# The value products of two query tiles in one run, and the transposes three units behind the scores, in an encoder's attention stage

## The chip, the core and the metric

The kernel runs on one core of one Trainium2 chip. The metric is the device time of one execution in microseconds (us), as the median of several runs. Engines: PE is the matmul engine (TensorE) and PEld its weight loads, DVE is VectorE, ACT is ScalarE, POOL is GpSimd, and SP is the queue from which most DMAs are issued.

## What is computed

One layer of an encoder for two request groups (1024 and 256 tokens of width 1024): modulated norm, one input projection, two attention branches side by side, a gated merge, an output projection, and a mixture of 32 experts. The change lies in the attention branches, 8 heads of width 64 each:

```python
sc = (jnp.einsum('bqhd,bkhd->bhqk', qn, k_nope, preferred_element_type=jnp.float32)
      + jnp.einsum('bqhr,bkr->bhqk', qr, k_rope, preferred_element_type=jnp.float32))
p = jax.nn.softmax(sc * scale, axis=-1).astype(v.dtype)
return jnp.einsum('bhqk,bkhd->bqhd', p, v)
```

That is the latent branch ("m"): every query of a group sees all its keys. The neighbourhood branch ("n") has a bias table and sees only a window of keys: for a tile of 128 queries, 384 columns of keys hold it, or 256 at the two ends.

## The kernel before, in words

**Units.** The attention stage is a list of 160 units. A unit is one head (x = 0 or 1 of a pair), one tile of 128 queries (qi) and all the keys that this tile sees. Units 0 to 63 are the m branch of the long group (1024 columns each), 64 to 127 its n branch (384 columns, 256 for qi 0 and 7), 128 to 159 the short group (256 columns, m and n by turns). Sixteen units (8 query tiles by 2 heads) use the tiles of one job, which holds queries, keys, values and bias tables and is loaded by `Job.load` (L807 to L857).

**What a unit does.** `scores` (PE, L895) fills one of two PSUM buffers. `maximum` (DVE, L903 for m, L907 with the bias for n) takes the row maximum, `exp` (ACT, L913) the exponentials and their sum, `normalize` the reciprocal (DVE, L916) and the scaling (POOL, L917). `transpose` (PE, L927; copies back by ACT and DVE, L929) turns the probabilities round, 128 columns at a time. `pv` (PE, L945) multiplies those of the two heads of a pair by the values: the two heads write the two halves of the PE array (64 columns each), by turns, 16, 12 or 8 products of 128 columns in each head-pair run of m, interior n or narrow units. The trace has two PE records per product. When the odd query tile is done, ACT (L951) and DVE (L952) split the product tile in two, and SP stores it (L954).

**Order.** No scheduler is at work: each engine executes in the order in which the loop below emits. In turn i it emits scores and maximum of unit i, transposes of unit i - LOOK, exp and normalize of unit i, then `pv`, then the loads that a table has for this i, then 2 or 3 matmuls of a filler. The filler (`piece_gates`) is the gate projection of the first 512 tokens, 16 groups of 24 matmuls (L678); at the end of a group ACT copies the result (L682) and SP stores it (L683), and about every nine units ACT and DVE split the next weights in two (L654, L655). The filler is used up at unit 145.

**Slots.** All tiles of 128x1024 come from one first-in-first-out list of 49 slots (`sl.get`, `sl.put`). A put is made when the last use has been emitted, not when it is done; so whoever gets a slot waits for its last reader, which may be a store that is still in flight. A unit's probabilities hold a slot from `maximum` to `pv`.

The loop reads, before:

```python
if u:
    u.exp()
    u.normalize()
if z and z.x:
    pv(units[i - LOOK - 2], z)
```

Of the kernel before, what the change touches and what calls it, by code (L numbers as in the profile page):

```python
# [86 lines left out]
def f32(x):  # L87
    return x.bitcast(F32)


def v3(t, k):
    return t.rearrange("p (k n) -> p k n", k=k)
# [3 lines left out]
def kernel(ctx, tc, A, out_p, out_s, upto=99, dbg=None):  # L96
# [311 lines left out]
    def work(g, *after):  # L408


        gi = order.index(g)
        def ahead():
            if gi + 1 < len(order):
                order[gi + 1].split()
            if gi + 2 < len(order):
                order[gi + 2].load()

        g.run(ahead)
        ada_step()
        for f in after:  # L420
            f()
            ada_step()
        g.put()
# [371 lines left out]
    def fill(n):  # L795

        while filled[0] < n:
            filled[0] += 1
            if next(fill_it, True):
                break  # L800
# [132 lines left out]
    def pv(a, b):  # L933

        half = a.qi % 2
        key = (a.kind, a.p, a.job.g)
        if half == 0:
            oacc[key] = fps["o"][:, oturn[0] % 2, :]
            oturn[0] += 1
        o = oacc[key]  # L940
        cs = slice(half * 128, half * 128 + 128)
        for i in range(0, a.n, 128):
            w = min(128, a.n - i)
            for u in (a, b):
                PE.matmul(o[64 * u.x:64 * u.x + 64, cs], u.job.vat(u.t0 + i // 128, u.h, w), v3(u.P, 8)[:w, i // 128, :],  # L945
                          start=(i == 0), stop=(i + 128 >= a.n), tile_position=(0, 64 * u.x), skip_group_check=True)
        sl.put(a.P, b.P)
        if half:
            os = sl.get(F32R)
            t = os[:, :512].rearrange("p (x n) -> p x n", x=2)  # L950
            S.copy(t[:, 0], o)  # L951
            V.tensor_sub(t[:, 1], o, f32(t[:, 0]))  # L952
            tk = (SP if a.job.g else 0) + (a.qi - 1) * 128
            SY.dma_start(ao_d[a.kind][:, a.p * 128:a.p * 128 + 128, tk:tk + 256].rearrange("x r n -> r x n"), f32(t))  # L954
            sl.put(os)
        if b.last:
            sl.put(*b.job.t)

    jobs = [Job(kind, 0, p) for kind in "mn" for p in range(4)]
    units = []  # L960
# [4 lines left out]
    for i in range(2):  # L965
        sj = [Job(kind, 1, i) for kind in "mn"]
        jobs += sj
        seqs = [[Unit(j, p, qi, x) for p in (2 * i, 2 * i + 1) for qi in range(2) for x in range(2)] for j in sj]
        for s in seqs:
            s[-1].last = True  # L970

        for k in range(0, 8, 2):
            units += seqs[0][k:k + 2] + seqs[1][k:k + 2]
    work(lat[1], latent_sq, rope_key)
    work(qq[0], latent_stat)
    work(qq[1])
# [90 lines left out]
    fps["o"] = psO.tile([128, 2, 256], F32, name="o")  # L1067
    fps["p"] = pool("psF", bufs=1, space=PSUM, stack=astack)

    LOOK = 2  # L1070
    LO, LS = (5, 5, 5, 5, 4, 4, 4), (4, 6, 4, 7)
    load_at = {16 * j + LO[j]: [jobs[j + 1]] for j in range(7)}
    load_at.update({16 * 7 + LS[0]: [jobs[8]], 16 * 7 + LS[1]: [jobs[9]], 128 + LS[2]: [jobs[10]], 128 + LS[3]: [jobs[11]]})
# [2 lines left out]
    merge = Merge()  # L1076
    for i in range(n + LOOK + 2):
        u = units[i] if i < n else None
        w = units[i - LOOK] if 0 <= i - LOOK < n else None
        z = units[i - LOOK - 1] if 0 <= i - LOOK - 1 < n else None  # L1080
        if u:
            u.scores()
            u.maximum()
        if w:
            w.transpose(0)
            w.transpose(1)
        if u:
            u.exp()
            u.normalize()
        if z and z.x:  # L1090
            pv(units[i - LOOK - 2], z)
        for j in load_at.get(i, []):
            j.load()
        fill(384 * (i + 1) // NF)
        if i == NP:
            merge.prime()
        if i == NP + 4:
            merge.ws[0].split()
            merge.out_load(0)
        if i > NP:  # L1100
            next(scaling, None)
# [658 lines left out]
```

## Time and profile before

| | |
|---|---|
| runs | 1855.3, 1858.37, 1858.37 us; median 1858.37 |
| profiled execution | 1854.83 us, of it 1853.1 us from the first instruction to the last |
| mean granted PE clock | 0.973 of full |
| busy: PE, DVE, ACT, POOL | 1743.1 (94%), 1001.4 (54%), 838.8 (45%), 319.0 us (17%) |

Times in the trace count from the first instruction. Busy PE includes matmuls whose ends overlap, so a PE that is busy throughout may still start its instructions in a slower or a faster rhythm; that rhythm is read from the start times in the timeline. The attention stage lies from about 480 to 906 us.

### The profile page before, as it was taken

How to read it: one execution, taken by the hardware profiler on the slowest of the kernel's cores; microseconds unless marked ns; L12 is line 12 of the kernel's file. 1: busy time of each engine (PE TensorE's matmuls, PEld its weight loads, DVE VectorE, ACT ScalarE, POOL GpSimd, SP SyncE). 2: the span in 40 equal slices, each digit the busy share in tenths (PEclk: the TensorE clock that was granted, in tenths of full speed). 3: DMA queues.
4: the chain of work that ended last, by engine and by line, in shares of the span. 5: the costliest groups of instructions: out<-in, count | busy, mean ns of one | idle time of the engine just before them, and what ended most of it. 6: DMA issues, size and time to landing. Idle time of an engine off the chain costs nothing.

```text
span 1853.1 us, 27078 instructions
## 1 busy us (share of the span) xinstructions
PE 1743.1 (94%) x9874; PEld 1357.6 (73%) x9874; DVE 1001.4 (54%) x1674; ACT 838.8 (45%) x1391; POOL 319.0 (17%) x329
## 2 busy tenths in 40 slices
PE   5999999999999999999899999699999999999991
PEld 4787777998888888767688877567676676766760
DVE  6324422111455655444357466777777777777764
ACT  6222222321455555666533213366556565655642
POOL 0010210000122222322333000111111111111110
PEclk9989999999999999999899999799999999999995
DMA  9335676536714442878977356899999999999916
GB/s 349 109 115 168 222 264 221 191 91 165 152 55 112 115 121 86 232 214 230 297 251 224 132 216 235 327 359 360 361 365 360 362 356 361 358 356 364 349 36 242
DMA packets 268848, 439.47 MB, mean 237 GB/s; under 512 B 31928, under 2 KB 131592, under 8 KB 268712
## 3 DMA queue, kind: packets, MB, share of 16 engines
q1 hardware_dynamic: 252008, 389.45, 62.8%
q0 software_dynamic: 13824, 37.77, 7.3%
q10 hardware_dynamic: 2880, 10.49, 1.4%
q8 instruction: 79, 1.29, 0.3%
q14 instruction: 57, 0.47, 0.1%
HBM read 367.53 MB, written 82.67 MB: 243 GB/s over the span
## 4 chain that ended last, share of the span: by engine, by line
PE 84%; DVE 5%; DMA 5%; issue 2%; ACT 2%; SPq 1%; POOL 1%; DVEq 0%; POOLq 0%; ACTq 0%; another core or an unknown queue 0%
PE ph L1540 19%; PE pg L432 13%; PE py L1566 11%; PE s L895 6%; PE pw L1303 5%; PE fp L766 5%; PE fp L678 4%; PE o L945 4%; PE tp L927 4%; PE pg L599 3%; PE pt L1527 2%; PE pg L341 1%; PE pg L557 1%; PE pt L1553 1%; DMA x_d<-s,idx 1%
## 5 line engine op out<-in xcount | busy, mean ns | idle before, releaser
L1540 PE MATMUL ph<-s,s 128*128 128x512 f32 x1536 | 377.0, 401 | 1.4 <-DVE s L1530 1.2
L1399 ACT CAST s<-s 128x1024 fp32r<-128x1024 f32 x256 | 265.9, 1055 | 194.2 <-PE ph L1540 193.9
L1540 PEld LDWEIGHTS ph<-s,s 128*128 128x128 f32 x1536 | 286.4, 188 | 73.8 <-issue 13.9
L1400 DVE TENSOR_TENSOR s<-s,s 128x1024 fp32r<-128x1024 f32 x256 | 304.5, 1221 | 63.7 <-ACT s L1399 57.4
L432 PE MATMUL pg<-s,s 128*128 128x512 f32 (+1 forms) x1416 | 270.2, 351 | 7.8 <-ACT s L182 4.2
L432 PEld LDWEIGHTS pg<-s,s 128*128 128x128 f32 x1416 | 226.8, 190 | 53.0 <-ACT s L182 4.9
L1566 PE MATMUL py<-s,aT 128*128 128x512 f32 x512 | 225.1, 592 | 0.7 <-ACT aT L1555 0.7
L917 POOL TENSOR_SCALAR s<-s,m 128x1024 f32<-128x1024 f32 (+2 forms) x160 | 122.8, 767 | 438.5 <-DVE m L916 363.6
L1566 PEld LDWEIGHTS py<-s,aT 128*128 128x128 f32 x512 | 94.8, 190 | 108.2 <-issue 100.0
L895 PE MATMUL s<-s,s 96*128 96x512 f32 (+2 forms) x592 | 147.7, 368 | 1.8 <-ACT s L913 1.4
L913 ACT ACTIVATE s<-s,m 128x1024 f32<-128x1024 f32 (+2 forms) x160 | 124.9, 781 | 46.6 <-DVE m L903 27.3
L929 ACT COPY s<-tp 128x512 f32<-128x512 f32 (+2 forms) x160 | 78.2, 488 | 120.5 <-PE tp L927 116.9
L895 PEld LDWEIGHTS s<-s,s 96*128 96x128 f32 (+1 forms) x592 | 109.9, 190 | 27.9 <-ACT s L913 2.3
L678 PE MATMUL fp<-s,s 128*128 128x512 f32 x384 | 126.4, 430 | 2.8 <-ACT s L682 2.6
L927 PE MATMUL tp<-ident,s 128*128 128x128 f32 x752 | 110.4, 275 | 9.8 <-POOL s L917 9.4
L183 DVE TENSOR_TENSOR s<-s,s 128x1024 fp32r<-128x1024 f32 x31 | 37.7, 1224 | 148.7 <-ACT s L182 137.0
L1303 PE MATMUL pw<-s,s 128*128 128x512 f32 x480 | 118.0, 400 | 0.0
L766 PE MATMUL fp<-s,s 128*128 128x512 f32 (+1 forms) x576 | 114.0, 359 | 2.8 <-DMA s<-ao_m 1.4
L903 DVE TENSOR_REDUCE m<-s 128x1 f32<-128x1024 f32 (+1 forms) x80 | 85.0, 1062 | 51.6 <-PE s L895 50.2
L1572 POOL DMA_INDIRECT x_d<-s,idx x32 | 71.7, 2242 | 231.1 <-DVE s L1571 116.1
L766 PEld LDWEIGHTS fp<-s,s 128*128 128x128 f32 x576 | 96.5, 191 | 20.1 <-DMA s<-ao_m 2.1
L927 PEld LDWEIGHTS tp<-ident,s 128*128 128x128 f32 x752 | 89.3, 141 | 25.3 <-POOL s L917 15.9
(225 smaller groups left out, 2012.3 us busy)
## 6 DMA issues: line engine op xcount, KB each, us to landing
s<-in_expert_w SPq DMA_DIRECT2D x384, 512.0 KB
s<-in_w_in SPq DMA_DIRECT2D x47, 512.0 KB
s<-in_ada_w POOLq DMA_DIRECT2D x32, 512.0 KB, 6.1
s<-nak_d SPq DMA_DIRECT2D x40, 256.0 KB
s<-in_x_prompt SPq DMA_DIRECT2D x16, 512.0 KB
s<-in_ada_w SPq DMA_DIRECT2D x16, 512.0 KB
s<-gate_d SPq DMA_DIRECT2D x16, 512.0 KB
gate_d<-s SPq DMA_DIRECT2D x16, 384.0 KB
```

The lines of the kernel that those rows point to most:

```text
L432: PE.matmul(p[:m, :CHUNKS[c][1]], g.at(a, j, 0, m), b.at(j, c), start=(j == 0 and n == 0), stop=(j == KD - 1 and n == 2))
L678: PE.matmul(p, w.at(a, j), b.at(j, 0), start=(n == 0), stop=(n == 23))
L766: PE.matmul(p[:, :w], b.ws[i].at(u, x * 4 + j), o[:, v, :w], start=(m == 0), stop=(m == 11))
L895: PE.matmul(u.s[:, b, :u.w], a, c, start=(n == 0), stop=(n == len(ops) - 1))
L913: S.activation(u.out, u.src, AF.Exp, bias=u.m[:, 0:1], scale=u.sign, accum_out=u.m[:, 1:2])
L917: G.tensor_scalar(u.P[:, :u.n], u.P[:, :u.n], u.m[:, 2:3], 1.0, op0=OP.mult, op1=OP.mult)
L927: PE.transpose(tp[:w, i // 128, :], u.P[:, b * 512 + i:b * 512 + i + w], ident)
L1303: PE.matmul(b.p, x[b.c].at(k, b.c, b.k), w[:, k % 2, :], start=(k + i == 0), stop=(k == 7 and i == 2))
L1399: S.copy(hi, r)
L1400: V.tensor_sub(lo, r, f32(hi))
L1540: PE.matmul(p, a[:, 2 * q + k, :], v3(w, 2)[:, k, :], start=(q + k + i == 0), stop=(q == 3 and k == 1 and i == 2))
L1566: PE.matmul(p, b.aT_[:, k, :], w[:, hb * 512:hb * 512 + 512], start=(k == 0), stop=(k == 3))
```

## The change

Units of the short group are listed four of m, then four of n, where it was two and two, so that the two query tiles of a pair of heads follow each other. LOOK goes from 2 to 3. And `pv` is called only after the odd query tile, for both query tiles one behind the other.

```diff
-        for k in range(0, 8, 2):
-            units += seqs[0][k:k + 2] + seqs[1][k:k + 2]
+        for k in range(0, 8, 4):
+            units += seqs[0][k:k + 4] + seqs[1][k:k + 4]
...
-    LOOK = 2
+    LOOK = 3
...
-        if z and z.x:
-            pv(units[i - LOOK - 2], z)
+        if z and z.x and z.qi % 2:
+
+            for k in (4, 2):
+                pv(units[i - LOOK - k], units[i - LOOK - k + 1])
```

`z` is unit i - LOOK - 1. The number of instructions is the same on every engine. What moves shows in three places.

On PE, at the first products of the first job (o is the product tile, s24 and s27 the probabilities of units 0 and 1, s33 and s29 those of units 2 and 3, fp the filler), before:

```order
L945 MATMUL o_3905<-s24_3916,s38_3503 64x128
L945 MATMUL o_3905<-s27_3932,s38_3503 64x128
L678 MATMUL fp_3922<-s36_472,s26_3807 128x512
L678 MATMUL fp_3922<-s2_438,s22_3808 128x512
L678 MATMUL fp_3922<-s5_535,s26_3807 128x512
L895 MATMUL s_4046<-s21_3497,s39_3491 128x512
```

and now:

```order
L945 MATMUL o_3905<-s27_3932,s38_3503 64x128
L945 MATMUL o_3905<-s24_3916,s38_3503 64x128
L945 MATMUL o_3905<-s27_3932,s38_3503 64x128
L945 MATMUL o_3905<-s33_3950,s38_3503 64x128
L945 MATMUL o_3905<-s29_3965,s38_3503 64x128
L945 MATMUL o_3905<-s33_3950,s38_3503 64x128
```

The products of the second pair stand right behind those of the first, with no filler and no scores between.

On DVE at unit 108 (L907 writes the unit's probabilities slot, L916 is the reciprocal, L952 the split of a product tile; the words in brackets are what the row waits for, DMAHW being the completion of a DMA), before:

```order
L952 TENSOR_TENSOR s3_7382<-o_3905,s3_7382 128x256 [waits Activation_49]
L907 ISA s45_7392,m_7393<-s_7389,s42_6888 128x384 [waits PE_49,Pool_49]
L907 ISA m_7393 128x1
L916 RECIPROCAL m_7393<-m_7393 128x1 [waits Activation_49]
L907 ISA s13_7409,m_7410<-s_7406,s20_6886 128x384 [waits PE_49,Pool_49]
```

and now:

```order
L952 TENSOR_TENSOR s26_7394<-o_3905,s26_7394 128x256 [waits Activation_49]
L907 ISA s6_7404,m_7405<-s_7401,s28_6877 128x384 [waits DMAHW7_49,PE_49,Pool_49]
L907 ISA m_7405 128x1
L916 RECIPROCAL m_7405<-m_7405 128x1 [waits Activation_49]
L907 ISA s34_7420,m_7421<-s_7417,s20_6879 128x384 [waits PE_49,Pool_49]
```

The slot s6 of unit 108 is the one that the gate store of turn 100 reads (`gate_d<-s6_7243` on SP, behind the 15 loads of the last n job), so the row has a DMA to wait for. Before, that store's slot went to the gate copy of turn 109 on ACT.

On SP around the loads of the short group's first two jobs (the store L954 of a product tile stood between them), and on ACT at turn 123 (L654 is the split of the filler's weights), now:

```order
L844 DMA s21_7596<-vml_d 128x2x256 [waits DMAHW7_49,PE_49,Pool_49]
L807 DMA s40_7631<-naq_d 64x4x256 [waits DMAHW0_49]
...
L857 DMA s26_7645<-in_sbias 128x384 [waits DMAHW2_49]
L683 DMA gate_d<-s29_7650 128x512 [waits DMAHW3_49,Activation_49]
...
L951 CAST s20_7763<-o_3905 128x256 [waits PE_49]
L654 CAST s29_7768<-s45_7485 128x1024 [waits DMAHW5_49,DMAHW3_49]
L929 COPY s41_7707<-tp_7780 128x384 [waits PE_49,Pool_49]
```

L654 of turn 123 writes s29, which the gate store of turn 118 reads. Before, the slot of that store went to the product tile of turn 126 (L951), and L654 of turn 123 waited for its weights alone.

## Rows read from the trace of the kernel before

**Rows 1.** Windows: us, then busy us (instructions) of PE, PEld, DVE, ACT, POOL, PE clock, DMA

```profile
480.00:740.00 260.00, 260.00 (x2147) 220.78 (x2145) 147.87 (x232) 137.77 (x240) 74.46 (x69) 1.00 0.42 106
740.00:880.00 140.00, 131.51 (x958) 103.06 (x957) 65.87 (x247) 93.50 (x263) 41.17 (x76) 1.00 0.85 226
880.00:906.00 26.00, 19.88 (x142) 14.02 (x141) 10.80 (x42) 16.47 (x54) 14.70 (x29) 0.87 0.86 286
```

**Rows 2.** Timeline of PE in the m units: start, length, engine, line, tile, count

```profile
602.02 1.04 PE L927 MATMUL tp<-ident,s 128*128 128x128 f32 x8
602.99 1.97 PE L945 MATMUL o<-s,s 128*64 128x128 f32 x32
604.89 0.73 PE L678 MATMUL fp<-s,s 128*128 128x512 f32 x2
...
606.84 1.04 PE L927 MATMUL tp<-ident,s 128*128 128x128 f32 x8
607.63 0.94 PE L678 MATMUL fp<-s,s 128*128 128x512 f32 x3
```

**Rows 3.** Timeline of PE in the n units

```profile
751.88 0.88 PE L945 MATMUL o<-s,s 128*64 128x128 f32 x12
752.69 0.97 PE L678 MATMUL fp<-s,s 128*128 128x512 f32 x3
```

**Rows 4.** Timeline of DVE, n units 107 and 108; in brackets its idle time before

```profile
811.68 0.55 DVE L907 CUSTOM_DVE_ANT_0 s<-s,s 128x384 f32<-128x384 f32 x1
...
813.01 0.17 DVE L916 RECIPROCAL m<-m 128x1 f32<-128x1 f32 x1 [0.77 <-ACT s L913]
813.13 0.56 DVE L907 CUSTOM_DVE_ANT_0 s<-s,s 128x384 f32<-128x384 f32 x1
```

**Rows 5.** Timeline of DVE: maxima of units 77 to 80, 99, 100, 111 and 128

```profile
754.16 0.56 DVE L907 CUSTOM_DVE_ANT_0 s<-s,s 128x384 f32<-128x384 f32 x1 [0.49 <-PE s L895]
756.48 1.23 DVE L655 TENSOR_TENSOR s<-s,s 128x1024 fp32r<-128x1024 f32 x1 [0.77 <-ACT s L654]
757.62 0.42 DVE L907 CUSTOM_DVE_ANT_0 s<-s,s 128x256 f32<-128x256 f32 x1
...
759.31 0.41 DVE L907 CUSTOM_DVE_ANT_0 s<-s,s 128x256 f32<-128x256 f32 x1
760.55 0.42 DVE L907 CUSTOM_DVE_ANT_0 s<-s,s 128x256 f32<-128x256 f32 x1
...
796.21 0.55 DVE L907 CUSTOM_DVE_ANT_0 s<-s,s 128x384 f32<-128x384 f32 x1
797.69 0.56 DVE L907 CUSTOM_DVE_ANT_0 s<-s,s 128x384 f32<-128x384 f32 x1
...
820.12 0.41 DVE L907 CUSTOM_DVE_ANT_0 s<-s,s 128x256 f32<-128x256 f32 x1
...
852.02 0.42 DVE L903 TENSOR_REDUCE m<-s 128x1 f32<-128x256 f32 x1
```

**Rows 6.** Timeline of SP and ACT: last n job's loads, gate store of turn 100, its waiter

```profile
796.77 1.09 SPq L807 DMA_DIRECT2D s<-naq_d  x2
...
808.33 0.33 SPq L683 DMA_DIRECT2D gate_d<-s  x1
...
818.02 0.58 ACT L682 COPY s<-fp 128x512 f32<-128x512 f32 x1 [2.09 <-DMA gate_d<-s]
```

**Rows 7.** Timeline of SP and ACT: the short group's loads, gate store of turn 118, turn 126

```profile
827.17 0.63 SPq L807 DMA_DIRECT2D s<-mq_d  x1
...
832.50 0.38 SPq L844 DMA_DIRECT2D s<-vml_d  x1
...
835.27 1.25 SPq L807 DMA_DIRECT2D s<-naq_d  x2
...
843.85 0.33 SPq L683 DMA_DIRECT2D gate_d<-s  x1
...
849.61 0.35 ACT L951 CAST s<-o 128x256 fp32r<-128x256 f32 x1
```

## The prediction

> **What bounds the kernel now.** The page comes first; it says that PE is busy most of the span, and that is an average. The windows by stage say where [rows 1]: in the m units (480 to 740 us) PE is busy for all of 260.00 us at full clock; in the n units and the head of the short group (740 to 880) for 131.51 of 140.00; in the tail after the filler (880 to 906) for 19.88 of 26.00, at clock 0.87. So a microsecond saved on PE is worth a microsecond in the first stage only.
>
> What sets the pace in the n units the timeline of DVE shows [rows 4]. Its maximum is followed by ACT's exponential, DVE waits 0.77 us for that, takes the reciprocal, and only then, being in order, starts the next maximum: 1.45 us from maximum to maximum (811.68 to 813.13). For narrow units it is 1.24 (759.31 to 760.55); with a split of a product tile in between 1.69 (757.62 to 759.31), so 0.45 for the split; and where the filler's weights are split, DVE waits 0.77 for ACT and works 1.23, together 2.00 [rows 5]. I call this the loop. The rest of the stage is lost to what keeps the loop waiting.
>
> **The change part by part. Fewer runs of products.** The number of products stays; the runs fall from 80 to 40. The price of a run is read from PE's start times [rows 2]. From transposes straight to filler is 0.79 us (606.84 to 607.63), from transposes to products 0.97 (602.02 to 602.99): 0.18 more. Products to filler take 1.90 for 32 records (602.99 to 604.89), and 0.81 for 12 in the n units (751.88 to 752.69) [rows 3]: 0.0545 per record, and 0.156 that doesn't depend on the number. So a run costs 0.18 + 0.16 = 0.34 us. In the m units 16 runs go, on a PE without gaps: **-5.4**. If the price were nil, 0; if all 40 runs counted, -13.6. I take the m part here, and read the others from their own stages.
>
> **The n units, 64 to 100.** Before, maxima 80 to 100 took 37.14 us (760.55 to 797.69) [rows 5]. The loop alone would want 14 wide units at 1.45, 6 narrow at 1.24, five product splits at 0.45 and two weight splits at 2.00: 34.0. With 8 runs fewer on PE per 32 units and one more unit between scores and transposes, DVE can come nearer to the loop: 3.1 per 20 units is 5.6 over 36. It can't all come: ACT also copies transposes and filler, and stores of the gate wait behind loads here too (at turns 68 and 84), which may take up to 2 us each. Bounds 0 and -5.6; I take **-3**, about the middle.
>
> **The gate store of turn 100.** Slots go round first in, first out, so putting the probabilities back two units later shifts who gets which. Now the slot that the store of turn 100 reads is taken by the maximum of unit 108, on DVE, in the middle of the loop; before, it went to ACT's copy of the filler at turn 109, which waited 2.09 us for it (to 818.02) [rows 6]. The store is issued by SP behind the 15 loads of the last n job. Before, the first of these started at 796.77, 0.56 behind the maximum of unit 99 (796.21) [rows 5, 6], the store at 808.33, and it had landed at 818.02: 21.25 after the first load, 9.69 after its own issue. The loads reuse slots whose last reader, the store of a product tile, now comes one turn later, so I set the same 0.56 + 21.25 = 21.8 from the maximum of unit 100. By the loop unit 108 is due 8 x 1.45 + 2 x 0.45 + 2.00 = 14.5 after unit 100. DVE would wait 7.3, and behind it its reciprocals, maxima and product splits; then ACT's exponentials, and PE once both score buffers are full. Unit 111 comes three units later, 21.8 + 2 x 1.45 + 1.24 = 25.95 after unit 100, where it came after 22.43 (797.69 to 820.12): **+3.5**. If the store were in time, 14.5 + 4.14 = 18.6: -3.8.
>
> **The gate store of turn 118.** Now ACT's split of the weights at turn 123 (L654) takes the slot that this store reads; behind it on ACT stand the copies of transposes and the exponentials, and DVE's half of the split waits for it. SP loads the short group's first two jobs from 827.17 on [rows 7]. Between them it paused from 832.88 (832.50 + 0.38) to 835.27 for a store of a product tile that no longer stands there, and issued the gate store at 843.85: 16.68 after the first load, less the pause 14.3. With 0.56 ahead it is issued 14.9 after the maximum of unit 116. It had landed before 849.61, when the next user of the slot ran: at most 5.8 after issue; I take 5, since that cast waited for its products last. So it lands 19.9 after unit 116. By the loop the split is due after 7 x 1.45 + 2 x 0.45 = 11.05 and most of a unit more, 12.3. Units 111 to 116 take 3 x 1.24 + 2 x 1.45 + 0.45 + 2.00 = 9.1, and from the split to unit 128 there are 2.00 and four units, 2 x 1.45 + 2 x 1.24 + 0.45 = 5.8. From 111 to 128: 9.1 + 19.9 + 2.0 + 5.8 = 36.8, where it was 31.9 (820.12 to 852.02) [rows 5]: **+4.9**. Without the wait it would be 29.2: -2.7.
>
> **Short group and tail.** With the filler, units 128 to 145, four runs fewer are 4 x 0.34 = -1.4; a smaller wait of the same kind (unit 144 takes the slot that the store of turn 136 reads) may give back half: **-0.7**. In the tail the normalization on POOL gets a unit more of slack, but the last two pairs' products come one behind the other at the very end: bounds -4 and +2, I take **-1**, the middle.
>
> **The sum.** -5.4 - 3 + 3.5 + 4.9 - 0.7 - 1 = -1.7 on the profiled execution's 1854.83, so 1853. The median of the runs is 3.5 above that execution; against it 1858.4 - 1.7 is about **1857 us**. A measurement of this kernel tells 0.2% from no change, 3.7 us, so the forecast is no difference that can be told. Its own range is 1849 to 1863: the n units and the tail at their ends, and each landing some us off.
>
> **Rivals. The stores land in time.** SP could start its loads earlier, or the stores could pass quicker when the loads ahead are done. Against it: 9.69 us from issue to landing in rows 6; for it: at most 5.8 in rows 7, and a landing there that no row fixes. Then the two terms are -3.8 and -2.7 in place of +3.5 and +4.9, the third wait goes too (-1.4), and the sum is -5.4 - 3 - 3.8 - 2.7 - 1.4 - 1 = -17.3: **1841 us**, chance 0.27. Beside it stands a rule of the Trainium skill, "DMA: Bandwidth & Descriptors", section "Anatomy of one DMA — SWDGE (gpsimd) path": about 2.0 us fixed for a DMA plus its bytes at 436 GB/s. For these 256 KB that makes an estimate of 2.6 us, and unit 108 would still wait for the issue, but little. The row with 9.69 disagrees with it for a store behind 15 loads, and the measurement decides; the row with at most 5.8 leaves it open.
>
> **The double run holds the loop (slower).** In the n units a run has 24 records instead of 12: 12 x 0.0545 = 0.65 us longer between the transposes ahead of it and what is behind it on PE, the next scores. ACT's cast of the product tile waits for its end, with exponentials behind it. If the next scores aren't ready by the time the loop wants them, each of 20 double runs (16 in the n units, 4 in the short group) delays it by 0.65: +13, less 2.6 by which the two store waits shrink, **1867 us**. It decides where PE is behind the loop by over two score buffers, about 2.9 us. Against it: PE idles 8.5 of 140 us there, and the unit of look-ahead more. Chance 0.09.
>
> **The price isn't per run.** If PE's change of tile shape costs the same in sum, because the double run has it inside, the -5.4 goes: **1862 us**, chance 0.04.
>
> **The clock falls in the tail.** The tail's granted clock is already a mean of both levels: 19.88 x 0.87 = 17.3 us of work at full clock. All of it at half speed would be 34.6 instead of 26: +8.6, **1866 us**. What speaks for it is that more of the products now stand behind the last transposes and waits; against it that these 26 us were at full speed for most of the time. Chance 0.07. The Trainium skill, "TensorE: Matmul & The Clock Gate", section "Part 4: PE-mode transpose", says that transposes don't count as busy in the same way, which would favour this rival; in rows 1 the m units, transposes among them, ran at 1.00.
>
> **How the numbers follow.** The forecast has 0.53, of which 0.14 lie more than 0.2% below the median of before, 0.32 within and 0.07 above. The stores in time are faster, 0.27; the other three slower or at the edge, 0.20. So faster 0.41, same 0.32, slower 0.27. Faster and slower cases both count, so the range reaches from the first rival to the last, 1840 to 1866, and leaves out the double run and the far side of the stores in time.
>
> **What would show it.** Right: runs of products with 64 records in the m units and 24 in the n units, half as many; DVE at unit 108 and ACT's L654 at turn 123 idle for some 7 us each, ended by the gate store's DMA; maxima 80 to 100 in some 35.5 us. Wrong: no such idle time (first rival); gaps ahead of the maxima ended by PE behind each double run (second); an m stage no shorter (third); a clock under 0.7 in the tail (fourth).

## The result, and the profile after

The changed kernel takes 1872.71 us (median of 4 runs, 1869.79 to 1872.74) against 1856.94 us before (4 runs): ratio 1.0086, 95% interval 1.0071 to 1.0101. It is 16 us slower; the forecast was 1857, the range ended at 1866.

The second stretch of [rows 1] in the changed kernel (columns as there):

```profile
740.00:880.00 140.00, 114.51 (x839) 93.65 (x837) 57.91 (x213) 82.41 (x225) 36.04 (x65) 0.94 0.74 197
```

There PE was busy for 131.51 us at clock 1.00; now it is for 114.51 at 0.94. What it waited for stands on the page, in the group of the scores (busy, mean ns of one, idle time ahead and what ended most of it), now and before:

```profile
L895 PE MATMUL s<-s,s 96*128 96x512 f32 (+3 forms) x592 | 150.1, 373 | 26.6 <-DVE m L907 21.2
```

```profile
L895 PE MATMUL s<-s,s 96*128 96x512 f32 (+2 forms) x592 | 147.7, 368 | 1.8 <-ACT s L913 1.4
```

PE waits for DVE, since in the n units a score buffer is free only when its unit's maximum is done; so the next question is what DVE and ACT waited for. In their timeline three idle times end on a gate store's DMA, one on DVE and two on ACT (the half of the split on DVE, L655, then waits 11.06 us for ACT):

```profile
820.59 0.56 DVE L907 CUSTOM_DVE_ANT_0 s<-s,s 128x384 f32<-128x384 f32 x1 [6.18 <-DMA gate_d<-s]
```

```profile
860.46 1.04 ACT L654 CAST s<-s 128x1024 fp32r<-128x1024 f32 x1 [10.44 <-DMA gate_d<-s]
898.84 0.47 ACT L913 ACTIVATE s<-s,m 128x256 f32<-128x256 f32 x1 [2.17 <-DMA gate_d<-s]
```

These are unit 108, turn 123 and unit 144, the three places that the prediction named. The times of the maxima say what each stretch lost. They are counted from unit 0: it starts at 482.57 us before and at 486.94 after, ahead of everything that the change touches, and in the profiles of the experiments, all alike up to there, at anything from 482.31 to 487.83. So 4.4 of the 17.9 us between the two profiles are not the change's.

| stretch | forecast, us | measured, us |
|---|---|---|
| m units, 0 to 64 | -5.4 | -3.3 |
| n units 64 to 100 | -3 | -0.25 |
| 100 to 111 (store of turn 100) | +3.5 | +5.1 |
| 111 to 128 (store of turn 118) | +4.9 | +12.3 |
| 128 to 146 | -0.7 | +1.7 |
| from 146 on | -1 | -2.1 |
| sum | -1.7 | +13.5 |

Of the last row 0.6 us lies ahead of the maximum of unit 159 and 1.4 behind it. Behind it all kernels of this document run the same code but for the last transposes and products, and their profiles still differ by -4.3 to +1.2 us from that of the kernel before. So the experiments are compared by the maxima too, and not by their medians alone.

### The profile page after: what moved, and what is told of

Read it like the earlier page. It is cut to its first block, busy times and chain, and to the rows that moved or that the text cites. A ratio compares the mean times of both kernels' runs of the same rounds, so it can differ in the third digit from the quotient of the medians.

```text
span 1871.0 us, 27083 instructions
## 1 busy us (share of the span) xinstructions
PE 1735.8 (93%) x9874; PEld 1361.1 (73%) x9874; DVE 1000.7 (53%) x1674; ACT 837.5 (45%) x1391; POOL 320.0 (17%) x329
## 4 chain that ended last, share of the span: by engine, by line
PE 73%; DVE 6%; DMA 6%; issue 3%; ACT 2%; SPq 0%; POOL 0%; DVEq 0%; POOLq 0%; ACTq 0%; another core or an unknown queue 0%
PE ph L1542 18%; PE py L1568 11%; PE pg L432 9%; PE s L895 5%; PE pw L1305 5%; PE fp L766 5%; PE o L945 4%; PE tp L927 4%; PE fp L678 3%; PE pg L599 3%; PE pt L1529 1%; DMA gate_d<-s 1%; ACT s L913 1%; DVE s L907 1%; PE pt L1555 1%
## 5 line engine op out<-in xcount | busy, mean ns | idle before, releaser
L1542 PEld LDWEIGHTS ph<-s,s 128*128 128x128 f32 x1536 | 287.3, 189 | 74.1 <-issue 13.9
L895 PE MATMUL s<-s,s 96*128 96x512 f32 (+3 forms) x592 | 150.1, 373 | 26.6 <-DVE m L907 21.2
L1573 DVE SCALAR_TENSOR_TENSOR s<-py,slots,s 128x512 f32<-128x512 f32 x64 | 48.1, 751 | 101.8 <-PE py L1568 98.3
```

Of the source, the lines that this page charges most:

```text
L895: PE.matmul(u.s[:, b, :u.w], a, c, start=(n == 0), stop=(n == len(ops) - 1))
L1542: PE.matmul(p, a[:, 2 * q + k, :], v3(w, 2)[:, k, :], start=(q + k + i == 0), stop=(q == 3 and k == 1 and i == 2))
```

## The experiments

Theory W: slots that a store still reads are taken too early, and the waits for it cost the time. Rival R: the runs of double length hold the loop, and the waits only take time that would be lost anyway. Each kernel was timed against the kernel before; the table gives the ratio and, from the profile, how much later than before (from unit 0 on) four maxima come.

| kernel | median, us | ratio (95%) | unit 64 | 100 | 128 | 159 |
|---|---|---|---|---|---|---|
| the change | 1872.71 | 1.0086 (1.0071, 1.0101) | -3.3 | -3.5 | +13.9 | +15.0 |
| e1 change, late put of gate slots | 1854.24 | 1.0000 (0.9991, 1.0008) | -3.3 | -1.2 | +0.4 | +0.9 |
| e2 before, late put of gate slots | 1855.75 | 1.0009 (0.9997, 1.0020) | 0.0 | +0.6 | -1.3 | -1.1 |
| e3 LOOK = 3 alone | 1866.29 | 1.0070 (1.0055, 1.0085) | -0.9 | -1.5 | +11.8 | +11.4 |
| e4 double runs alone | 1861.62 | 1.0041 (1.0029, 1.0053) | -2.2 | -0.4 | +5.7 | +6.6 |
| e5 change, both late puts | 1846.34 | 0.9951 (0.9936, 0.9965) | -3.4 | -5.1 | -7.8 | -8.9 |
| e6 before, both late puts | 1850.70 | 0.9975 (0.9967, 0.9984) | 0.0 | -0.6 | -2.7 | -2.8 |
| e7 double runs in m alone, both late puts | 1845.29 | 0.9946 (0.9933, 0.9958) | -3.3 | -4.6 | -7.1 | -8.8 |
| e8 double runs but in m, both late puts | 1846.94 | 0.9957 (0.9944, 0.9969) | -0.9 | -2.4 | -5.1 | -6.2 |
| e9 change, a load later | 1863.35 | 1.0044 (1.0027, 1.0061) | -3.3 | -4.5 | +5.9 | +6.6 |
| e10 change, another load later | 1859.06 | 1.0020 (1.0008, 1.0031) | -3.3 | -3.4 | +2.7 | +3.8 |
| e11 LOOK = 3 alone, both late puts | 1848.26 | 0.9957 (0.9941, 0.9973) | -0.9 | -1.9 | -4.4 | -6.6 |
| e12 e7 with both loads later | 1848.25 | 0.9952 (0.9934, 0.9970) | -3.3 | -4.5 | -7.1 | -9.3 |

**e1, the slot of the gate store kept for nine turns more.**

```diff
+        held = []
...
-                        sl.put(t)
+                        held.append(t)
+                        if len(held) == 2:
+                            sl.put(held.pop(0))
```

> The change, with the slot of each gate store given back one filler group (nine turns) later, so that no instruction of ACT or DVE takes it while the store is in flight. Theory W (the waits for the gate stores cost the time: 6.18 us at unit 108, 10.44 us at turn 123, 2.17 us at unit 144): the three idle times go and the time falls to 1854 to 1859 us, no slower than before. Rival R (the runs of products of double length hold the loop, and the waits only take time that would be lost anyway): 1866 us or more.

1854.24 us: all three waits are gone, and with them the whole loss. But it is no faster than before either, where the prediction's first rival gave 1841 for this case. Its trace has two waits on ACT for stores of product tiles: 2.64 us ahead of the split at turn 95, where the change itself has a wait of that kind on DVE (2.04 us), and one that is new, at turn 127 (L955 is the change's L951; the edits move the line numbers):

```profile
851.78 0.37 ACT L955 CAST s<-o 128x256 fp32r<-128x256 f32 x1 [3.86 <-DMA ao_n<-s]
```

**e2, the same edit on the kernel before.**

> The kernel before with the same edit of the slot. Both theories: only the wait of 2.09 us for the store of turn 100 goes; 1854 to 1858 us, the same as before. If it falls by more, the edit has a worth of its own that must be taken off the first run's.

No difference that can be told by the median, as expected, and 1.1 us by the maxima: the edit by itself is worth next to nothing there, so what e1 wins back, the whole 0.86%, is the waits' and that of what follows each of them.

**e3 and e4, the two halves of the change.** e3 is the kernel before with LOOK = 3; e4 is the changed kernel with LOOK = 2.

> LOOK = 3 alone: single runs of products, short group listed two and two. By the order of slots the store of turn 100 is again waited for at unit 108, and that of turn 118 by the maximum of unit 124. Theory W: two waits of about 6 and 10 us, 1867 to 1873 us, though no run of products is longer. Rival R: 1855 to 1859 us.

> Runs of double length and the list by fours, with LOOK = 2. The store of turn 100 is waited for at unit 108; that of turn 118 has the same successor as before (the cast of a product tile at turn 126). Theory W: one wait of about 6 us, 1857 to 1863 us. Rival R: the runs hold the loop without the unit of slack, 1868 us or more.

e3 decides against R: with single runs throughout, it is 0.7% slower, and waits on DVE at unit 108 and unit 124, as the order of the slots said:

```profile
817.88 0.56 DVE L907 CUSTOM_DVE_ANT_0 s<-s,s 128x384 f32<-128x384 f32 x1 [6.04 <-DMA gate_d<-s]
857.47 0.56 DVE L907 CUSTOM_DVE_ANT_0 s<-s,s 128x384 f32<-128x384 f32 x1 [7.33 <-DMA gate_d<-s]
```

The median is 1 us under the expected 1867. e4, with one wait (4.06 us at unit 108) and double runs, lies in the range that W gave. Either half alone shifts the slots far enough for a wait.

**e5 and e6, the product tiles' slots kept as well** (two product tiles longer), in the changed kernel and in the one before:

```diff
-            sl.put(os)
+            ohold.append(os)
+            if len(ohold) > 2:
+                sl.put(ohold.pop(0))
```

> The change, with the slots of the gate stores given back nine turns later and those of the product tiles' stores two product tiles later. In the first run 2.64 us (turn 95) and 3.86 us (turn 127) were still lost to stores of product tiles. Theory W (stores in flight): both go, 3 to 6.5 us below the kernel before (about 1848 to 1851 us). Rival: something else then ends the idle time, no faster than the kernel before.

> The kernel before with the same two edits of slots. Nothing of over 0.4 us was left to gain there: within 2 us of the kernel before.

e5 is 9 us below the kernel before, more than expected. e6 missed: the kernel before gains 4.6 us by its median, of which the maxima show 2.8 (2.1 of them between units 100 and 111, where the wait of 2.09 us of [rows 6] is gone); in its profile another 4.3 us lie behind unit 159, where the edits change nothing. So the change without waits for stores is worth 1846.34 - 1850.70 = -4.4 us, by the maxima -8.9 + 2.8 = -6.1.

**e7, e8 and e11, which part of the change is worth what.** All with both late puts. e7 has double runs in the m units of the long group alone, e8 everywhere but there, e11 nowhere:

```diff
-        if z and z.x and z.qi % 2:
-
-            for k in (4, 2):
+        if z and z.x and (z.qi % 2 or (z.kind == "n" or z.job.g)):
+            for k in (2,) if (z.kind == "n" or z.job.g) else (4, 2):
                 pv(units[i - LOOK - k], units[i - LOOK - k + 1])
```

> As e5, but runs of double length in the m units of the long group alone; n units and short group keep single runs and the list by twos. Theory D (in the n units a double run delays the scores behind it and costs about what it saves, 0.5 to 1 us at a time): another 2 to 5 us faster than e5, 1844 to 1848 us. Rival S (the 24 runs saved there are worth their 0.34 us each): up to 8 us slower than e5.

> As e5, but double runs in the n units and the short group alone; m units single. The 3.3 us that the m units gained are lost: 3 us slower than e5 by both theories; by theory D also slower than e6 or the same (0 to 3 us), by rival S faster than e6 by 3 us or more.

> LOOK = 3 with single runs and the list by twos, and both late puts: what the unit of look-ahead is worth without store waits. From e7 and e8: m units -0.95, n units and tail about -5.3 against the kernel before, so 1847 to 1849 us where e5 had 1846.3, 2 us slower than the m-double kernel. If it is within 1 us of e7, double runs are worth nothing anywhere.

Behind unit 64 the four kernels with LOOK = 3 gain the same, whatever their runs: -5.6 (e5), -5.5 (e7), -5.3 (e8), -5.6 (e11), against -2.8 for e6. So the 24 runs saved outside the m units are worth nothing, and cost nothing; theory D and its rival S of e7's expectation both fall. By its median e8 is 3.8 us faster than e6, as S asked, but e11, which has none of those double runs, gains as much there: it is the look-ahead. The third unit of look-ahead is worth 2.8 us behind unit 64. In the m units double runs are worth 2.4 (-3.3 or -3.4 against -0.9). By medians e5, e7, e8 and e11 can hardly be told apart.

**e9 and e10, the store issued ahead of the loads.** Each moves one job's loads by one turn, from ahead of the gate store on SP to behind it; who takes which slot stays as in the change.

```diff
-    LO, LS = (5, 5, 5, 5, 4, 4, 4), (4, 6, 4, 7)
+    LO, LS = (5, 5, 5, 5, 4, 4, 5), (4, 6, 4, 7)
```

(e9; e10 has LS = (4, 7, 4, 7) instead.)

> The change with the last n job's loads emitted at turn 101, behind the gate store of turn 100 on SP, where they stood ahead of it. Unit 108 still takes the slot of that store. Theory W: the store is issued some 10 us earlier, the idle 6.18 us at unit 108 go, 5 us faster than the change (that is 9 to 10 us slower than the kernel before, by medians about 0.5%); unless the loads are then late for unit 112. Rival: the wait is for something else in unit 108, and nothing changes.

> The change with the second job of the short group loaded at turn 119, behind the gate store of turn 118 on SP; the split of the weights at turn 123 still takes that store's slot. Theory W: the store stands behind 9 loads instead of 20, is issued 8 to 11 us earlier, and the 10.44 us at turn 123 go: 9 to 11 us faster than the change (4 to 6 us slower than the kernel before). Rival: the split then waits for its weights, whose load stands behind the same loads, and little changes.

In e9 the store of turn 100 leaves SP at 796.25 and not behind the loads; unit 108 runs at 810.25 with no idle time ahead of it (SP and DVE):

```profile
796.25 0.33 SPq L683 DMA_DIRECT2D gate_d<-s  x1
796.69 1.09 SPq L807 DMA_DIRECT2D s<-naq_d  x2
```

```profile
810.25 0.55 DVE L907 CUSTOM_DVE_ANT_0 s<-s,s 128x384 f32<-128x384 f32 x1
819.92 0.42 DVE L907 CUSTOM_DVE_ANT_0 s<-s,s 128x256 f32<-128x256 f32 x1 [2.50 <-DMA ao_n<-s]
```

At unit 128 e9 is 8.0 us ahead of the change, more than the 5 expected (by medians 8.0 us behind the kernel before), although 2.50 us go to the store of a product tile at unit 112 (second row of DVE). e10, likewise, runs the split of turn 123 without a wait (SP and ACT):

```profile
841.52 0.42 SPq L683 DMA_DIRECT2D gate_d<-s  x1
```

```profile
847.28 1.05 ACT L654 CAST s<-s 128x1024 fp32r<-128x1024 f32 x1
```

and is 11.2 us ahead at unit 128 (by medians 3.7 us behind the kernel before, just under the 4 to 6 expected). So the place of one store on SP is worth 8 us, and that of the other 11, what follows the waits included.

**e12, e7 with both loads later.**

> e7 with the loads of turns 100 and 118 at turns 101 and 119, behind the gate stores. By theory W nothing waits for a gate store there any more in e7, so within 2 us of it (1843 to 1847 us); faster by over 2 us only if loads or stores hold something that the traces do not show.

1848.25 us, 1 us above the expected end and with an interval that overlaps that of e7: nothing more is gained. e5, e7, e8, e11 and e12 all beat both the kernel before and the changed one; between them the medians do not decide.

## Why the prediction was wrong

**The mechanism of the store waits was right, and the sizes were not.** Both store waits bit where they were put, unit 108 came 22.06 us after unit 100 (798.53 to 820.59) where 21.8 was forecast, and the wait there was 6.18 where 7.3 was. The forecast fell on the sum: the two stretches cost 17.4 us instead of 8.4, and the gains that were to pay for them were 3.6 instead of 8.4.

**The step that failed most is "less the pause 14.3"**, in the term of the store of turn 118 (+4.9, measured +12.3), with what that term leaves out behind it. SP's rows at turn 118 (start, length; compare [rows 7]):

```profile
838.30 0.63 SPq L807 DMA_DIRECT2D s<-mq_d  x1
...
849.09 4.03 SPq L857 DMA_DIRECT2D s<-in_sbias  x4
855.03 0.33 SPq L683 DMA_DIRECT2D gate_d<-s  x1
```

The pause for the product tile's store is gone, but from the first load to the gate store SP still needs 16.73 us (16.68 before): the four last loads take 4.03 us (2.83 before), and the gap behind them is 1.91 us (0.86 before). I had taken the pause off as if it alone stood in SP's way. What SP waited for at these two places, between the first load and the gate store (us in total, times, longest), now and before:

```profile
SPq L683 <- DMA s<-nak_d: 1.8, 1, 1.8
SPq L857 <- DMA s<-naq_d: 1.3, 2, 0.7
SPq L857 <- DMA s<-nak_d: 0.8, 1, 0.8
```

```profile
SPq L683 <- DMA s<-nak_d: 0.8, 1, 0.8
SPq L857 <- DMA s<-nak_d: 0.7, 1, 0.7
```

The last loads and the store waited 3.9 us for earlier loads to land, where it had been 1.5: 2.4 us more, as much as the pause that went. This is read from one trace each; no run tries it by itself. The store lands 5.43 us after its issue (5 was taken), so 22.7 us after unit 116 and not 19.9: 2.8 of the 7.4 us by which this term was too small.

**The rest of it is the pace behind the wait: a loop forecast too fast, and the clock.** The forecast let the loop go on at its full pace as soon as a wait ended. The windows of the two waits and of the 5 us behind each (columns as above):

```profile
814.00:821.00 7.00, 1.67 (x10) 1.12 (x8) 0.82 (x2) 0.48 (x1) 0.58 (x1) 0.97 1.11 344
821.00:826.00 5.00, 3.56 (x12) 2.87 (x13) 1.56 (x9) 3.12 (x9) 1.65 (x3) 0.50 0.24 85
850.00:861.00 11.00, 2.91 (x17) 2.23 (x15) 0.42 (x1) 0.56 (x2) 0.59 (x1) 0.87 1.06 267
861.00:866.00 5.00, 2.71 (x9) 2.42 (x10) 2.92 (x9) 3.02 (x8) 0.76 (x2) 0.50 0.25 82
```

PE stood idle for most of 7 and of 11 us, and then ran at 0.50, the 1.2 GHz level, until a few us later (1.00 from 831 to 850 us). Its rows:

```profile
821.21 0.80 PE L895 MATMUL s<-s,s 128*128 128x256 f32 x2 [5.54 <-DVE m L907]
...
823.88 1.65 PE L678 MATMUL fp<-s,s 128*128 128x512 f32 x3 [1.23 <-ACT s L682]
```

The scores of a narrow unit take 0.80 us where 0.41 is usual (829.18), three filler matmuls 1.65 where 0.96. The loop, bound by DVE and ACT at full clock, becomes bound by PE: unit 111 waits 1.20 us for its scores. 108 to 111 takes 5.51 us (4.14 forecast), 111 to 116 takes 11.64 (9.1), and from the split of turn 123 to unit 128 it is 9.84 (7.8): 1.4, 2.5 and 2.0 us, 5.9 in all. The double runs are not to blame: e3, with single runs and a like wait at unit 108, takes 5.51 and 11.71 us for the first two. But the clock is not all of it either. In e5, with no such wait and the clock at 1.00 from 800 to 855 us, the three take 4.62, 10.94 and 8.09 us (e11, single runs: 4.63, 10.93 and 8.09). So 2.6 of the 5.9 us are a loop forecast too fast (between units 111 and 116, for one, two splits of a product tile fall where one was counted), and the other 3.3 us are the clock together with whatever else follows a wait; they are not measured apart. The forecast had a rival for the clock, but put it into the tail, where it was 0.87 (898 to 925 us, behind the filler), as before.

**The m units: right price, forgotten cover.** From products to filler a double run takes 3.65 us:

```profile
615.74 3.71 PE L945 MATMUL o<-s,s 128*64 128x128 f32 x64
619.39 0.73 PE L678 MATMUL fp<-s,s 128*128 128x512 f32 x2
```

By the price per record, 64 x 0.0545, the rest is 0.16, as in [rows 2, 3] (a product has two records; a single run has 16 products in the m units, 6 in the interior n units and 4 in narrow ones, and the 12 and 8 in the description of the kernel before are records); and where PE has no gaps, eight units take 30.63 us where they took 31.34, 0.355 per run saved (0.34 forecast). The Trainium skill names a possible cause ("TensorEngine Tiling (Array Packing)", Key Properties: a change of tiling mode drains the engine); the rows here show the price and not the cause. But three times PE now waits for DVE's copy of a unit's second transposes:

```profile
503.99 0.66 PE L927 MATMUL tp<-ident,s 128*128 128x128 f32 x4 [1.19 <-DVE s L929]
...
538.46 0.66 PE L927 MATMUL tp<-ident,s 128*128 128x128 f32 x4 [0.66 <-DVE s L929]
...
646.43 0.66 PE L927 MATMUL tp<-ident,s 128*128 128x128 f32 x4 [0.42 <-DVE s L929]
```

Each comes 3.3 us behind a split of the weights on DVE (500.68, 535.16 and 643.12 us), in one of the stretches of four units that now hold no products: 2.27 us of the 5.4 go back. Single runs had covered DVE there: e3 and e11 have no such wait. That 5.4 less 2.27 comes near the measured 3.3 is partly luck. On PE itself the scores of unit 64 start 2.4 us earlier after unit 0 than before, and 0.1 earlier in e3 and e11; the table goes by unit 64's maximum on DVE, which comes 0.95 earlier in these two without any double run. So the double runs are worth 2.3 to 2.4 us there, and about 0.7 us of what is lacking stays open.

**The n units: the middle of two bounds was too much.** Of the -3 came -0.25. Without waits for stores (e5) it is -1.8, and e6 has -0.6 of this without the change; the 1.5 us between the change and e5 are one wait for a product tile's store ahead of the split at turn 95 (2.04 us, 0.52 in e5). e5 against e7 shows the runs saved there at nothing. The short group's term went wrong the same way, +1.7 us for -0.7: the wait at unit 144 is 2.17 us, and four runs fewer, priced at -1.4, are worth 0.4 at most (e5, units 128 to 146).

**The rivals.** The stores in time: e1 is that case for the gate stores and no faster than before; e5, where the product tiles' stores are out of the way too, is 9 us faster where the rival said 17. By its maxima e5 lacks 2.1 us in the m units, 1.2 in the n units up to 100, and 1.8 and 2.0 in the two stretches of the stores, where even without a wait the loop is slower than forecast. The Trainium skill's "DMA: Bandwidth & Descriptors", section "Anatomy of one DMA — SWDGE (gpsimd) path", by which a store would land 2.6 us after its issue (an estimate; the page fits it on DMAs of the gpsimd path, and these stores are issued by SP), is not borne out in the change either: it took 5.43 us at turn 118 behind 20 loads. The double run that holds the loop came nearest in its number (1867) and is not the cause (e3, e7). The price of a run held per run. The clock did fall, elsewhere.

## What to carry to other kernels

Where buffers go round first in, first out, a tile that is kept two turns longer gives everyone else a younger buffer: before quoting a gain, list for each store in flight who takes its buffer next, before and after the change, and how many DMAs stand ahead of the store on its queue. Keeping a stored tile out of the list for a while (e5), or issuing the store ahead of the next burst of loads (e9, e10: one number), cost no time that these runs can tell (e2; e12 against e7) and in the changed kernel is worth more (1872.71 to 1846.34 us with both late puts) than the change itself is without waits (4.4 to 6.1 us). And a wait of several us on a helper engine can cost more than its length, if the matmul engine stands still in it: count what follows at the lower clock (up to 3.3 us here).

## What was not expected of the hardware

The granted clock was 0.50 in the 5 us behind each of the two long waits, after PE had stood for 5.54 and 10.38 us, and 1.00 again by 831 and by 871 us; in e3, behind waits of 6.04 and 7.33 us on DVE and with no double runs, it was 0.50 as well at 818 to 823 us and at 857 to 862. And SP's row of loads for two jobs took 16.7 us from its first load to the store behind it with the pause in its middle and without, as its waits for its own earlier loads rose from 1.5 to 3.9 us.
